# A feed-forward input product in seven block products instead of eight, for three double groups of hidden units

## The chip, the cores and the metric

The kernel runs on one NeuronCore of a Trainium2 chip. The time is the device time of one execution in microseconds, as the median of several runs. Five engines work from queues of their own, in order: TensorE (PE in the profile; its weight loads are PEld), VectorE (DVE), ScalarE (ACT), GpSimd (POOL) and SyncE (SP), which issues the loads.

## The reference

One layer of a decoder trunk on 256 tokens of width 1024, all in float32. After the mixing part and the cross attention over a memory comes the feed-forward part, which the change is about, and the final norm:

```python
def reference(...):
    ...
    h = h + memory_cross_attention(rmsnorm(h, norm_x_g[l]), rmsnorm(mem, norm_mem_g[l]),
                                   wq_x[l], wkv_x[l], wo_x[l])
    hn = rmsnorm(h, norm_ffn_g[l])
    gu = hn @ w_ffn_in[l]
    h = h + (jax.nn.silu(gu[..., :FFN_HIDDEN]) * gu[..., FFN_HIDDEN:]) @ w_ffn_out[l]
    return rmsnorm(h, final_norm_g)
```

`hn` is 256 x 1024, `w_ffn_in` 1024 x 5632, `w_ffn_out` 2816 x 1024.

## The kernel before, in words

All weights lie in one array of 1 MB units in the order in which they are used (`plan`, `ORDER`). A unit is 128 partitions by 2048 columns. For nearly full float32 accuracy every weight unit is split into two parts: `hi` is the value rounded by a copy on ScalarE, `lo = raw - hi` is a subtraction. `prep` does this for one unit: it issues the load on SP's queue (L188), the copy on ScalarE in two pieces of 1024 columns (L194), and the subtraction of each piece (L198), 576 columns of it on VectorE and 448 on GpSimd. Two raw buffers and three of each part are in rotation, and `nxt` prepares two units ahead. Activations are split in the same way (`split`, L285 and L286). A product then takes three matmuls for each 128 x 128 block of activations against 512 columns: hi by hi, hi by lo, lo by hi (`mm3t`, L238 to L240).

The feed-forward part works on 11 hidden groups of 256 units. Group `o` has two input units `("I", o, kh)`, one for each half of the 1024 features, with 256 columns of the gate and 256 of the value side by side, and one output unit `("O", o)`. `ffn_in` accumulates a bank of 128 tokens by 512 columns over both input units for each token half `t`: four block products of 12 matmuls for a group. `gate` takes Silu of the gate half (L1089, scaled by the token's reciprocal norm `r`) and multiplies (L1091, scaled by `r` again). `turn_hid` turns the result with four transposes into one bank (L1099) and splits it. `out_part` accumulates the output in four banks, 24 matmuls for an output unit. Output unit `o-1` runs behind the input of group `o`.

Ahead of that, the residual `H` gets the product with `wo` (`pso`, from four prepared units, the last two in buffers B10, B11, B12 and B6), `add_h` adds it and sums squares (L918, L922), and `turn_h2` turns a quarter of H (L1064), multiplies with the gain (L1066) and splits it, with the lo part on GpSimd (L1068). `rstd2` makes the reciprocal norms (L293, L295) and only the gates need them.

The order of TensorE's instructions is the program's. On ScalarE, VectorE, GpSimd and SP a planner orders the instructions by its own estimates; each engine's queue then runs strictly in that order, and an instruction at its head that waits holds back all behind it. Only the last part after the products has a written order.

Of the kernel before, what the change touches and what calls it, by code (L numbers as in the profile page):

```python
# [24 lines left out]
EPS = 1e-6  # L25
# [15 lines left out]
V_MIX, V_X, V_MEM, V_FFN, V_HG, V_L0, V_L1 = (8 * i for i in range(7))  # L41


def plan():
    order = []

    def tgroup(name, base):
        return [("T", name, base + c * 512, kh) for c in range(2) for kh in range(2)]

    order += [("T", "w_in", 4096 + c * 512, kh) for kh in range(2) for c in range(2)]  # L50
    order += [("F", "w_in", 3 * 1024 + c * 256) for c in range(4)]
    for base in (5, 2, 0, 1, 6):
        order += tgroup("w_in", base * 1024)
    order += tgroup("w_in", 8 * 1024) + tgroup("w_in", 7 * 1024)
    order += tgroup("w_br_hgrn", 0) + tgroup("w_br_attn", 0)
    order += tgroup("w_out", 0)
    order += [("F", "wkv_x", c * 256) for c in range(4)]
    order += tgroup("wkv_x", 1024)[:2]
    order += [("F", "wq_x", c * 256) for c in range(4)]
    order += tgroup("wkv_x", 1024)[2:]  # L60
    order += tgroup("wo_x", 0)
    for j in range(NF // 2):
        order += [("I", j, 0), ("I", j, 1)]
        if j:
            order.append(("O", j - 1))
    order.append(("O", NF // 2 - 1))
    return order


ORDER = plan()  # L70


def lay(ws):
# [39 lines left out]
def bc(ap, n, axis):  # L113
    shape = list(ap.shape)
    shape.insert(axis, n)
    return ap.unsqueeze(axis).to_broadcast(shape)


def build(tc, A, out):
    nc = tc.nc  # L120
    V, SC, G, PE, SY = nc.vector, nc.scalar, nc.gpsimd, nc.tensor, nc.sync
    with ExitStack() as ctx:
# [3 lines left out]
        cp = pool("cp", 1)  # L126
        wr, wh, wl = pool("wr", 2), pool("wh", 3), pool("wl", 3)
# [114 lines left out]
        def by_k(w, k):  # L242
            return tuple(t.rearrange("p (k c) -> p k c", k=k) for t in w)
# [671 lines left out]
        def add_h(t, c, ps, scale, ssq):  # L915
            d = H[:, t, c * 512:(c + 1) * 512]
            if scale is None:
                V.tensor_tensor(d, ps, d, op=ALU.add)  # L918
# [3 lines left out]
            SC.activation(j, d, AF.Square, accum_out=ssq[:, t, c:c + 1])  # L922
# [129 lines left out]
        gfin = big("B4", "gfin", (128, 1024))  # L1052
        SY.dma_start(gfin, A["gfin"].to_broadcast([128, 1024]))
        H2 = big("P2", "H2", (128, 2, 8, 256), F32R)
        h2h, h2l = H2[:, 0], H2[:, 1]
        def wo_part(ps, t, c, kh):
            t_part(ps, wo[2 * c + kh], (oxh, oxl), t, kh)

        def turn_h2(t, c):
            ks, ts = slice(4 * c, 4 * c + 4), slice(t * 128, (t + 1) * 128)  # L1060
            bk = bank("h2T", (128, 4, 128))
            for j in range(4):
                k = 4 * c + j
                PE.transpose(bk[:, j], H[:, t, k * 128:(k + 1) * 128], ident)  # L1064
            g = t2("h2g", (128, 4, 128))
            V.tensor_tensor(g, bk, bc(gv[:, V_FFN + 4 * c:V_FFN + 4 * c + 4], 128, 2), op=ALU.mult)  # L1066
            SC.activation(h2h[:, ks, ts], g, AF.Copy)
            G.tensor_tensor(h2l[:, ks, ts], g, h2h[:, ks, ts].bitcast(F32), op=ALU.subtract)  # L1068

        todo = None  # L1070
        for t in range(2):
            for c in range(2):
                ps = mm.tile([128, 512], F32, name="pso", tag="mm")
                wo_part(ps, t, c, 0)
                if todo:
                    turn_h2(*todo)
                wo_part(ps, t, c, 1)
                add_h(t, c, ps, None, ssq2)
                todo = (t, c)


        ring = ("B7", "B14", "B10", "B11", "B12", "B6")
        X2 = (h2h, h2l)
        hid, acc, two, psi, hm = {}, {}, {}, {}, {}

        def gate(o, t):
            r, ps = two["r"][:, t:t + 1], psi.pop((o, t))
            g = t2("fg", (128, 256))
            SC.activation(g, ps[:, 0:256], AF.Silu, scale=r)  # L1089
            u = t2b("fu", (128, 256))  # L1090
            V.scalar_tensor_tensor(u, ps[:, 256:512], r, g, op0=ALU.mult, op1=ALU.mult)  # L1091
            hm[o, t] = u

        def turn_hid(o):
            bk = mm.tile([128, 2, 256], F32, name="hidT", tag="mm")
            for t in range(2):
                u = hm.pop((o, t))
                for j in range(2):
                    PE.transpose(bk[:, j, t * 128:(t + 1) * 128], u[:, j * 128:(j + 1) * 128], ident)  # L1099
            hd = big(ring[o % 6], "hid", (128, 2, 2, 256), F32R)  # L1100
            split(bk, hd[:, 0], hd[:, 1])
            hid[o] = hd

        def ffn_in(o, kh, t, w):
            if kh == 0:
                psi[o, t] = mm.tile([128, 512], F32, name="psi", tag="mm")
            t_part(psi[o, t], w, X2, t, kh)
# [11 lines left out]
        def ffn_out(o):  # L1119
            w = by_k(nxt(), 2)  # L1120
            for t in range(2):
                for c in range(2):
                    out_part(o, w, t, c)

        for u in ORDER[at[0]:-2]:
            if u[0] == "O":
                ffn_out(u[1])
                continue
            _, o, kh = u
            w = by_k(nxt(), 4)  # L1130
            for t in range(2):
                ffn_in(o, kh, t, w)
                if (o, kh, t) == (0, 0, 0):
                    turn_h2(1, 1)
                    two["r"] = rstd2(ssq2, "h2")
                if kh == 1:
                    gate(o, t)
            if kh == 0 and o:
                turn_hid(o - 1)

        n = NF // 2 - 1
        wa = by_k(nxt(), 2)
        wb = by_k(nxt(), 2)
        out_part(n - 1, wa, 0, 0)
        turn_hid(n)
        out_part(n - 1, wa, 0, 1)
# [8 lines left out]


        ssq3 = cp.tile([128, 5], F32, name="ssq3")
        hg3 = {i: big(ring[j], "hg3", (128, 512)) for j, i in enumerate(((0, 0), (0, 1), (1, 0)))}  # L1160
# [95 lines left out]
```

## Time and profile before

| | |
|---|---|
| median of 3 runs | 624.86 us (624.67 to 625.35) |
| the profiled execution | 625.08 us, span 623.1 us, granted clock 0.998 |
| TensorE busy | 615.1 us, 99% |
| VectorE busy | 395.6 us, 63% |
| ScalarE busy | 334.1 us, 54% |
| GpSimd busy | 371.5 us, 60% |

A group's row gives the line, the engine, the operation, output and inputs, shapes, count, then the busy time in us and the mean duration in ns, and the idle time before it with what ended it. A row of the timeline gives start and duration in us. In the chain of waits each row is a start and the time that it adds to the chain. The feed-forward part begins at about 431 us of the span and its products end at 615.

### The profile page before, as it was taken

How to read it: one execution, taken by the hardware profiler on the slowest of the kernel's cores; microseconds unless marked ns; L12 is line 12 of the kernel's file. 1: busy time of each engine (PE TensorE's matmuls, PEld its weight loads, DVE VectorE, ACT ScalarE, POOL GpSimd, SP SyncE). 2: the span in 40 equal slices, each digit the busy share in tenths (PEclk: the TensorE clock that was granted, in tenths of full speed). 3: DMA queues.
4: the chain of work that ended last, by engine and by line, in shares of the span. 5: the costliest groups of instructions: out<-in, count | busy, mean ns of one | idle time of the engine just before them, and what ended most of it. 6: DMA issues, size and time to landing. Idle time of an engine off the chain costs nothing.

```text
span 623.1 us, 8546 instructions
## 1 busy us (share of the span) xinstructions
PE 615.1 (99%) x3153; PEld 513.7 (82%) x3153; DVE 395.6 (63%) x691; ACT 334.1 (54%) x550; POOL 371.5 (60%) x296
## 2 busy tenths in 40 slices
PE   8999999999999999999999999999999999999995
PEld 7888888888877877778888888888888888888884
DVE  7589888979776875748846456754444444444433
ACT  7785554234376866727547556644543344434432
POOL 3888744556544564356857876656655665566553
PEclk9999999999999999999999999999999999999999
DMA  8754553334433333545454544453354455455511
GB/s 346 288 197 149 203 202 136 136 135 147 191 137 135 136 136 136 203 174 191 145 213 189 187 176 178 143 196 135 136 180 175 187 202 184 177 184 198 204 68 68
DMA packets 16890, 107.53 MB, mean 173 GB/s; under 512 B 2000, under 2 KB 2640, under 8 KB 4560
## 3 DMA queue, kind: packets, MB, share of 16 engines
q1 hardware_dynamic: 16128, 106.14, 46.9%
q10 hardware_dynamic: 720, 0.84, 0.4%
q8 instruction: 25, 0.41, 0.3%
q14 instruction: 17, 0.14, 0.1%
HBM read 105.92 MB, written 1.05 MB: 172 GB/s over the span
## 4 chain that ended last, share of the span: by engine, by line
PE 98%; DVE 0%; POOL 0%; issue 0%; POOLq 0%; DVEq 0%
PE pst L238 13%; PE pst L240 13%; PE pst L239 13%; PE psf L259 7%; PE psi L238 6%; PE psi L240 6%; PE psi L239 6%; PE psf L260 4%; PE acc L240 3%; PE acc L238 3%; PE acc L239 3%; PE lp L613 2%; PE psg L514 1%; PE pso L238 1%; PE pso L240 1%; PE pso L239 1%
## 5 line engine op out<-in xcount | busy, mean ns | idle before, releaser
L198 POOL TENSOR_TENSOR lo<-raw,hi 128x448 fp32r<-128x448 f32 x172 | 272.0, 1597 | 181.4 <-ACT hi L194 178.4
L194 ACT ACTIVATE hi<-raw 128x1024 fp32r<-128x1024 f32 (+1 forms) x194 | 196.2, 1037 | 161.1 <-PE pst L240 58.2
L198 DVE TENSOR_TENSOR lo<-raw,hi 128x576 fp32r<-128x576 f32 (+2 forms) x194 | 197.8, 1024 | 127.9 <-ACT hi L194 126.1
L238 PE MATMUL pst<-hi,XX 128*128 128x512 f32 x224 | 90.4, 404 | 0.0
L240 PE MATMUL pst<-hi,XX 128*128 128x512 f32 x224 | 87.4, 390 | 0.0
L239 PE MATMUL pst<-lo,XX 128*128 128x512 f32 x224 | 87.3, 390 | 0.0
L238 PE MATMUL psi<-hi,H 128*128 128x512 f32 x176 | 69.6, 395 | 0.0
L240 PE MATMUL psi<-hi,H 128*128 128x512 f32 x176 | 68.7, 390 | 0.0
L239 PE MATMUL psi<-lo,H 128*128 128x512 f32 x176 | 68.5, 389 | 0.0
L240 PEld LDWEIGHTS pst<-hi,XX 128*128 128x128 f32 x224 | 42.0, 188 | 9.0
L238 PEld LDWEIGHTS pst<-hi,XX 128*128 128x128 f32 x224 | 42.1, 188 | 8.8 <-issue 0.7
L239 PEld LDWEIGHTS pst<-lo,XX 128*128 128x128 f32 x224 | 42.1, 188 | 7.9
L240 PEld LDWEIGHTS psi<-hi,H 128*128 128x128 f32 x176 | 33.0, 188 | 7.1
L239 PEld LDWEIGHTS psi<-lo,H 128*128 128x128 f32 x176 | 33.1, 188 | 6.6
L238 PEld LDWEIGHTS psi<-hi,H 128*128 128x128 f32 x176 | 33.1, 188 | 6.5
L238 PE MATMUL acc<-hi,hid 128*128 128x512 f32 x86 | 33.6, 390 | 0.0
L240 PE MATMUL acc<-hi,hid 128*128 128x512 f32 x86 | 33.5, 389 | 0.0
L239 PE MATMUL acc<-lo,hid 128*128 128x512 f32 x86 | 33.5, 389 | 0.0
L1091 DVE SCALAR_TENSOR_TENSOR fu<-psi,r_h,fg 128x256 f32<-128x256 f32 x22 | 10.6, 483 | 25.1 <-ACT fg L1089 25.1
L1089 ACT ACTIVATE fg<-psi,r_h 128x256 f32<-128x256 f32 x22 | 10.4, 475 | 29.1 <-PE psi L240 29.1
L259 PE MATMUL psf<-H,hi 128*128 128x512 f32 x64 | 22.8, 400 | 0.0
L259 PE MATMUL psf<-XX,hi 128*128 128x512 f32 x64 | 22.6, 396 | 0.0
(336 smaller groups left out, 1199.4 us busy)
## 6 DMA issues: line engine op xcount, KB each, us to landing
raw<-w SPq DMA_DIRECT2D x94, 1024.0 KB, 4.8
raw<-w SPq DMA_DIRECT2D x4, 512.0 KB, 6.5
raw<-w SPq DMA_DIRECT2D x4, 256.0 KB, 4.0
H<-xtok SPq DMA_DIRECT2D x1, 1024.0 KB, 9.6
mraw<-mT SPq DMA_DIRECT2D x1, 1024.0 KB, 4.9
xraw<-xT SPq DMA_DIRECT2D x1, 512.0 KB, 6.5
gfin<-gfin SPq DMA_DIRECT2D x1, 512.0 KB, 3.7
out<-H SPq DMA_DIRECT2D x2, 256.0 KB, 2.0
```

The source lines that it names most:

```text
L194: SC.activation(hi[:, a], raw[:, a], AF.Copy)
L198: eng.tensor_tensor(lo[:, b], raw[:, b], hi[:, b].bitcast(F32), op=ALU.subtract)
L238: PE.matmul(ps, xh, h, start=first, stop=False)
L239: PE.matmul(ps, xh, l, start=False, stop=False)
L240: PE.matmul(ps, xl, h, start=False, stop=last)
L259: PE.matmul(ps, w[0][:, k, a], X2[:, :, k], start=k == 0, stop=False)
L260: PE.matmul(ps[:, 0], w[1][:, k, a], X2[:, 0, k], start=False, stop=k == 7)
L514: PE.matmul(pss[c][t], z[:, k, t * 128:(t + 1) * 128], ws[c][0][:, k], start=z is Xh and k == 0, stop=False)
L613: PE.matmul(ps[:, j], KS[:, a0 + j], QQ[:, a0 + j], start=True, stop=True)
L1089: SC.activation(g, ps[:, 0:256], AF.Silu, scale=r)
L1091: V.scalar_tensor_tensor(u, ps[:, 256:512], r, g, op0=ALU.mult, op1=ALU.mult)
```

## The change

Two neighbouring hidden groups `q` and `q+1` form a double group; there are three (2 and 3, 5 and 6, 8 and 9). For such a pair the input product is two token halves by two feature halves by two groups, eight block products. The new code computes it with Winograd's form of Strassen's scheme: seven block products of sums of blocks. `SEVEN` gives their order, P1, P2, P6, P7, P5, P3, P4. Products with plain operands are P1 (block 11 by token half 0, feature half 0), P2 (block 21, feature half 1); the others use sums. The groups 0, 1, 4, 7 and 10 keep the old form.

- `load_blocks` loads the four blocks of a double group into the fixed buffers B12, B6, B10 and B11 and forms the combination of 22 and 12 at once; `block` forms three more combinations in place (for P6, P5, P4). Each combination is two VectorE operations of 1024 columns (`both`). `BY_DMA` is false, so `less` isn't used.
- `halve` splits a unit or a block in one piece of 2048 columns (two pieces for the first two units): copy on ScalarE, subtraction on VectorE alone. Every fourth goes to a fixed pair of buffers in P1's place (`px`). GpSimd splits no weights from here on. `prep_u` prepares three units ahead.
- `token_sums` forms four sums of token blocks and splits them, on VectorE with copies on ScalarE.
- `ffn_product` runs one product into one of three banks (A, B, F), and copies partial sums of bank A away on ScalarE (`keep`) where a later step needs them; `whole` adds a kept sum to a bank on VectorE.
- The reciprocal norm is applied ahead of the transposes (`rstd_h2`, `add_h2`), and not in `gate`; the lo part of the turned tokens moves to VectorE. The units 0 to 3 run first for token half 0, then for half 1, with the transposes of half 1 before unit 3.
- The output units are spread among the products by `ffn_plan`, the turns by `TURNS`.

```diff
+SEVEN = ("P1", "P2", "P6", "P7", "P5", "P3", "P4")
+def ffn_plan():
...
+    out = two(0) + two(1)
+    out += seven(2, P2=[0], P5=[1]) + two(4)
+    out += seven(5, P2=[2], P7=[3], P5=[4]) + two(7)
+    out += seven(8, P2=[5], P7=[6], P5=[7])
+    out += two(10) + [("O", 8)]
+    return out + [("O", 9), ("O", 10)]
...
+LOADS = {0: (2,), 10: (5,), 22: (8,)}
+TURNS = {4: (0,), 8: (1,), 15: (2,), 18: (3,), 20: (4,), 27: (5,), 30: (6,), 32: (7,), 38: (8, 9)}
...
+        def halve(raw, n):
+            if n % 4 == 3:
+                hi, lo = px[:, 0:2048], px[:, 2048:4096]
...
+                SC.activation(hi[:, a], raw[:, a], AF.Copy)
+                V.tensor_tensor(lo[:, a], raw[:, a], hi[:, a].bitcast(F32), op=ALU.subtract)
...
+        def block(q, name):
...
+            if name == "P6":
+                both(blk["11"], blk["12"], blk["11"], ALU.add)
+            elif name == "P5":
+                both(blk["12"], blk["22"], blk["11"], ALU.subtract)
+            elif name == "P4" and not BY_DMA:
+                both(blk["21"], blk["21"], blk["11"], ALU.subtract)
...
-            G.tensor_tensor(h2l[:, ks, ts], g, h2h[:, ks, ts].bitcast(F32), op=ALU.subtract)
+                V.tensor_tensor(h2l[:, ks, ts], g, h2h[:, ks, ts].bitcast(F32), op=ALU.subtract)
...
+        def token_sums():
+            a11, a12, a21, a22 = (h2g[t, c] for t in range(2) for c in range(2))
...
+            V.tensor_tensor(a22, a21, a22, op=ALU.add)
+            V.tensor_tensor(s2, a22, a11, op=ALU.subtract)
+            V.tensor_tensor(a21, a11, a21, op=ALU.subtract)
+            V.tensor_tensor(a12, a12, s2, op=ALU.subtract)
...
+            if name == "P1":
+                keep("1", ps, t2("f1"))
+            elif name == "P2":
+                whole(q, 0, ps, "1")
+            elif name == "P6":
+                keep("2", ps, gf[:, 1024:1536])
+            elif name == "P5":
+                keep("4", ps, gf[:, 1536:2048])
+                whole(q + 1, 1, bank_of["F"], "4")
+            elif name == "P3":
+                psi[q + 1, 0] = ps
+                gate(q + 1, 0)
+            elif name == "P4":
+                whole(q, 1, ps, "2")
...
+        prep_u(3)
+        for n in range(4):
+            if n == 3:
+                turn_h2(1, hn1)
+            ffn_in(n, 0)
+        for n in range(4):
+            for q in LOADS.get(n, ()):
+                load_blocks(q)
+            ffn_in(n, 1)
+            if n == 0:
+                token_sums()
+            prep_u(n + 4)
+        for n in range(4, len(units) - 2):
+            for q in LOADS.get(n, ()):
+                load_blocks(q)
+            prep_u(n + 3)
+            for o in TURNS.get(n, ()):
+                turn_hid(o)
...
```

More of the change, by code (lines that the diff above doesn't have):

```diff
@@ L70, with seven, two @@
 ORDER = plan()
+SEVEN = ("P1", "P2", "P6", "P7", "P5", "P3", "P4")
+def ffn_plan():
+    def seven(q, **after):
+        out = []
+        for p in SEVEN:
+            out.append(("P", q, p))
+            out += [("O", o) for o in after.get(p, ())]
+        return out
+    def two(j):
+        return [("I", j, 0), ("I", j, 1)]
+    out = two(0) + two(1)
[4 more added lines that the diff above has]
+    return out + [("O", 9), ("O", 10)]
+FFN_PLAN = ffn_plan()
+BY_DMA = False
+LOADS = {0: (2,), 10: (5,), 22: (8,)}
+TURNS = {4: (0,), 8: (1,), 15: (2,), 18: (3,), 20: (4,), 27: (5,), 30: (6,), 32: (7,), 38: (8, 9)}
 def lay(ws):
@@ new lines, in both, with load_blocks @@
+        def both(out, x, y, op):
+            for i in range(2):
+                a = slice(1024 * i, 1024 * i + 1024)
+                V.tensor_tensor(out[:, a], x[:, a], y[:, a], op=op)
+        def load_blocks(q):
+            blk.clear()
+            for key, tag, c in (("22", "B12", (q + 1, 1)), ("12", "B6", (q + 1, 0)),
+                                ("11", "B10", (q, 0)), ("21", "B11", (q, 1))):
+                blk[key] = big(tag, "b" + key, (128, 2048))
+                SY.dma_start(blk[key], A["w"][where[("I",) + c]])
+            if BY_DMA:
+                less(blk["12"], blk["12"], (q + 1, 1))
+            else:
+                both(blk["12"], blk["22"], blk["12"], ALU.subtract)
@@ new lines, in less @@
+        def less(out, x, c):
+            SC.activation(out, x, AF.Copy, scale=-1.0)
+            G.dma_start(out, A["w"][where[("I",) + c]], accum_op=ALU.add)
+        def block(q, name):
+            if name == "P7" and BY_DMA:
+                less(blk["21"], blk["11"], (q, 1))
+            if name == "P6":
[4 more added lines that the diff above has]
+                both(blk["21"], blk["21"], blk["11"], ALU.subtract)
+            return blk[{"P1": "11", "P2": "21", "P6": "11", "P7": "12", "P5": "12", "P3": "22", "P4": "21"}[name]]
@@ L1056, in wo_part, with prep_u @@
+        units = FFN_PLAN
+        def prep_u(upto):
+            while made_u[0] <= min(upto, len(units) - 1):
+                n = made_u[0]
+                made_u[0] += 1
+                u = units[n]
+                if u[0] == "P":
+                    raw = block(u[1], u[2])
+                else:
+                    raw = wr.tile([128, 2048], F32, name="raw", tag="raw")
+                    SY.dma_start(raw, A["w"][where[u]])
+                pair[n] = halve(raw, n)
         def wo_part(ps, t, c, kh):
@@ L1070, in build, with add_h2, rstd_h2 @@
-        todo = None
+        ssq2 = cp.tile([128, 4], F32, name="ssq2")
+        v2 = cp.tile([128, 2], F32, name="v2")
+        r2 = cp.tile([128, 2], F32, name="r2")
+        h2g = {}
+        def add_h2(t, c, ps):
+            d = H[:, t, c * 512:(c + 1) * 512]
+            V.tensor_tensor(d, ps, d, op=ALU.add)
+            SC.activation(t2b("hjunk"), d, AF.Square, scale=1.0 / 32.0, accum_out=ssq2[:, 2 * t + c:2 * t + c + 1])
+        def rstd_h2(t):
+            V.tensor_scalar(v2[:, t:t + 1], ssq2[:, 2 * t:2 * t + 1], ssq2[:, 2 * t + 1:2 * t + 2], EPS,
+                            op0=ALU.add, op1=ALU.add)
+            G.tensor_tensor(r2[:, t:t + 1], v2[:, t:t + 1], nhalf[:, :1], op=ALU.pow)
+            hn = []
+            for c in range(2):
+                n = t2("hn")
+                SC.activation(n, H[:, t, c * 512:(c + 1) * 512], AF.Copy, scale=r2[:, t:t + 1])
+                hn.append(n)
+            return hn
@@ L1071, in build @@
+        hn0 = None
         for t in range(2):
@@ L1117, in out_part, with ffn_in @@
                      (o == 0 or home is not None) and k == 0, k == 1 and o >= NF // 2 - (2 if t and c else 1))
-        def ffn_out(o):
-            w = by_k(nxt(), 2)
+        def ffn_in(n, t):
+            _, o, kh = units[n]
+            if kh == 0:
+                psi[o, t] = mm.tile([128, 512], F32, name="psi", tag="mm")
+            t_part(psi[o, t], by_k(pair[n], 4), X2, t, kh)
+            if kh == 1:
+                gate(o, t)
+        SS = big("P0", "SS", (128, 2, 4, 4, 128), F32R)
@@ new lines, in tokens, with product @@
+        def tokens(name):
+            if name in ("P1", "P2", "P4"):
+                t, kh = {"P1": (0, 0), "P2": (0, 1), "P4": (1, 1)}[name]
+                return [[z[:, 4 * kh + k, t * 128:(t + 1) * 128] for k in range(4)] for z in X2]
+            i = {"P5": 0, "P6": 1, "P7": 2, "P3": 3}[name]
+            return [[SS[:, z, i, k] for k in range(4)] for z in range(2)]
+        def product(ps, name, w, first):
+            xh, xl = tokens(name)
+            for k in range(4):
+                for i, (x, z) in enumerate(((xh, w[0]), (xh, w[1]), (xl, w[0]))):
+                    PE.matmul(ps, x[k], z[:, k], start=first and k == 0 and i == 0, stop=k == 3 and i == 2,
+                              skip_group_check=not first)
@@ new lines, in build, with keep, whole, ffn_product @@
+        bank_of, kept = {}, {}
+        def keep(key, ps, home):
+            SC.activation(home, ps, AF.Copy)
+            kept[key] = home
+        def whole(q, t, ps, key):
+            c = t2("fc")
+            V.tensor_tensor(c, ps, kept.pop(key), op=ALU.add)
+            psi[q, t] = c
+            gate(q, t)
+        def ffn_product(n):
+            _, q, name = units[n]
+            w = by_k(pair[n], 4)
+            key = {"P1": "A", "P6": "A", "P5": "A", "P3": "A", "P2": "B", "P7": "F", "P4": "F"}[name]
+            first = name in ("P1", "P2", "P7")
+            if first:
+                bank_of[key] = mm.tile([128, 512], F32, name="pq" + key, tag="mm")
+            ps = bank_of[key]
+            product(ps, name, w, first)
+            if name == "P1":
[12 more added lines that the diff above has]
+                whole(q, 1, ps, "2")
@@ L1121, in ffn_out @@
+        def ffn_out(n):
+            w = by_k(pair[n], 2)
             for t in range(2):
                 for c in range(2):
[L1123 to L1139, printed above, removed]
+                    out_part(units[n][1], w, t, c)
@@ new lines, in build @@
+        prep_u(3)
[16 more added lines that the diff above has]
+                turn_hid(o)
+            u = units[n]
+            if u[0] == "I":
+                for t in range(2):
+                    ffn_in(n, t)
+            elif u[0] == "P":
+                ffn_product(n)
+            else:
+                ffn_out(n)
@@ L1143, in build @@
         n = NF // 2 - 1
-        wa = by_k(nxt(), 2)
-        wb = by_k(nxt(), 2)
+        wa, wb = (by_k(pair[len(units) - 2 + i], 2) for i in range(2))
         out_part(n - 1, wa, 0, 0)
@@ L1159, in build @@
         ssq3 = cp.tile([128, 5], F32, name="ssq3")
-        hg3 = {i: big(ring[j], "hg3", (128, 512)) for j, i in enumerate(((0, 0), (0, 1), (1, 0)))}
+        hg3 = {i: big(tag, "hg3", (128, 512)) for tag, i in zip(("B10", "B11", "B12"), ((0, 0), (0, 1), (1, 0)))}
         v3 = cp.tile([128, 3], F32, name="v3")
```

81 lines of the change are left out of this document (50 added, 31 removed).

## The prediction

> **What bounds the kernel now.** I read the head of the page first, then the chain of waits, then single matmuls in the timeline.
>
> ```profile
> span 623.1 us, 8546 instructions
> PE 615.1 (99%) x3153; PEld 513.7 (82%) x3153; DVE 395.6 (63%) x691; ACT 334.1 (54%) x550; POOL 371.5 (60%) x296
> PE 98%; DVE 0%; POOL 0%; issue 0%; POOLq 0%; DVEq 0%
> ```
>
> TensorE carries 98% of the chain: a matmul less is time less, as long as its operands are there in time. How much is one matmul?
>
> ```profile
> L239 PE MATMUL psi<-lo,H 128*128 128x512 f32 x176 | 68.5, 389 | 0.0
> 598.21 0.39 PE L240 MATMUL psi<-hi,H 128*128 128x512 f32 x1
> 598.89 0.39 PE L240 MATMUL psi<-hi,H 128*128 128x512 f32 x1
> 448.10 0.44 PE hidT L1099 x4
> 464.89 0.44 PE hidT L1099 x4
> 448.10:464.90 16.80, 16.80 (x78) 13.92 (x77) 7.68 (x9) 7.35 (x9) 10.03 (x6) 1.00 0.53 188
> ```
>
> The group row says 389 ns, but matmuls overlap: three starts lie between 598.21 and 598.89, so one costs 0.227 us. One hidden group of the feed-forward lasts 448.10 to 464.89, 16.79 us, which is 72 matmuls and four transposes (0.44): again 0.227. In that window (columns: length, then PE, PEld, DVE, ACT, POOL busy) VectorE works 7.68 of 16.80 us and the granted clock is 1.00. So before the change VectorE has more than half of its time free there. That is the reserve that the change spends.
>
> **The saving.** A double group takes eight block products of 12 matmuls now and seven after: 3 x 12 = 36 matmuls fewer (the build of both kernels has 2226 and 2190 matmuls 512 wide). 36 x 0.227 = 8.2 us off the chain. By the durations it would be 36 x 0.389 = 14.0, which the pitch refutes. Transposes stay at 44 and 16.
>
> **What VectorE gets.** Durations and the pitch between them:
>
> ```profile
> L198 DVE TENSOR_TENSOR lo<-raw,hi 128x1024 fp32r<-128x1024 f32 x2 | 2.4, 1216 | 0.0
> L286 DVE TENSOR_TENSOR hid<-hidT,hid 128x512 fp32r<-128x512 f32 x11 | 7.5, 685 | 1.4 <-ACT hid L285 1.4
> L286 DVE TENSOR_TENSOR oal<-ao,oah 128x256 fp32r<-128x256 f32 x8 | 3.3, 417 | 0.0
> 449.28 0.76 DVE L198 TENSOR_TENSOR lo<-raw,hi 128x576 fp32r<-128x576 f32 x1 [2.75 <-ACT hi L194]
> 449.95 0.68 DVE L286 TENSOR_TENSOR hid<-hidT,hid 128x512 fp32r<-128x512 f32 x1
> L198 DVE TENSOR_TENSOR lo<-raw,hi 128x576 fp32r<-128x576 f32 x172 | 174.3, 1016 | 123.4 <-ACT hi L194 121.7
> ```
>
> From 512 to 1024 columns 685 grows to 1216 ns, 1.04 ns a column; 2048 columns, which no run shows, come to 1216 + 1024 x 1.04 = 2.28 us. The 576-wide split takes 0.76 us alone at 449.28 but 1016 ns in the mean, where GpSimd splits beside it; after the change GpSimd splits nothing there, so I take the undisturbed values. Queued instructions overlap: 449.95 starts 0.67 us after a start of 0.76 us, so 0.08 to 0.09 less. Pitches: 2048 wide 2.20, 1024 wide 1.14, 512 wide 0.605, 256 wide 0.34.
>
> I then counted VectorE's queue in the build's order. In a double group it splits 7 products, 2 or 3 output units and 2 ordinary input units, and forms four block combinations (eight halves of 1024). From the first product of groups 5-6 to that of 8-9: 12 x 2.20 + 8 x 1.14 + 6 x 0.605 (three hidden splits, three sums with a kept bank) + 6 x 0.34 (gates) = 41.2 us, against 204 matmuls and 12 transposes on TensorE, 46.3 + 1.3 = 47.6. Between the first products of 2-3 and 5-6 it is 38 against 41.7. VectorE is the second engine everywhere, with 86 to 92% of TensorE's work, and in order.
>
> **Where it becomes the first: the opening.** The stretch begins when TensorE has turned the second token half (before unit 3), and ends with the lo part of the second hidden group, which the third matmul of output unit 1 reads. VectorE's queue there holds, without a gap in which it could wait for less: 8 splits of 2048 (17.6), 8 half combinations (9.1), 15 of 512 (two gains, two token splits, four token sums and their four splits, two hidden splits, one kept sum: 9.1) and 4 gates (1.4): 37.2 us, and about 0.5 where an instruction waits for the result of the one ahead. TensorE's work in it is 146 matmuls and 8 transposes: 33.1 + 0.9 = 34.0. The difference, 3.7 us, must appear as TensorE idling, most of it at P5 and at output unit 1, because the build puts hidden split 1 behind three block splits. After each stall the first matmul starts cold:
>
> ```profile
> 599.48 0.48 PE L238 MATMUL psi<-hi,H 128*128 128x512 f32 x1
> 599.79 0.40 PE L239 MATMUL psi<-lo,H 128*128 128x512 f32 x1
> ```
>
> Behind the transposes the first start takes 0.31 instead of 0.23, so three stalls add some 0.3. Term: +4.0. Bounds: 0, if TensorE's operands in fact never depend on the last of this queue; 6.8, if queued instructions did not overlap (35 x 0.08 = 2.8 more). I stay at the queue sum, since the overlap stands in the rows.
>
> The Trainium skill, in VectorE: DVE Perf Modes, section The DRAIN you can't avoid, says that the next operation does not start before the pipe of the last is empty. The trace disagrees by the 0.08 us shown.
>
> **What is hidden.** The rstd now stands ahead of the transposes instead of in the gate:
>
> ```profile
> 431.32 0.69 DVE L918 TENSOR_TENSOR H<-pso,H 128x512 f32<-128x512 f32 x1 [1.62 <-PE pso L240]
> 432.11 0.63 ACT L922 ACTIVATE hjunk<-H 128x512 f32<-128x512 f32 x1 [1.74 <-DVE H L918]
> 433.31 0.70 POOL L295 TENSOR_TENSOR r_h<-v__4128,nhalf 128x2 f32<-128x2 f32 x1 [0.83 <-DVE v__4128 L293]
> 443.07 1.05 ACT L194 ACTIVATE hi<-raw 128x1024 fp32r<-128x1024 f32 x1
> ```
>
> For the second token half: add 0.69, square with its readout 0.8, sum 0.17, power 0.70, two scalings 1.3, handovers: 4.1 us; unit 3's split stands ahead of it on ScalarE (2048 wide, 1.9 from 1.05 for 1024) and on VectorE (2.2), so up to 6.5. Cover: three half units of 12 matmuls, 8.2 us. Nothing, and 1 to 2 us if unit 3's load comes late. The first half has 5.4 us of matmuls over 4.1. ScalarE: 42 splits x 1.8 and some 30 copies and gates more, about 105 us of the stage's 176: not the bound. GpSimd loses 66 splits, off the chain: 0. Keeping P1, P6, P5 takes three copies a double group on ScalarE, each behind one product or output unit (2.7 us and more): 0.
>
> **Loads.** Same bytes, but a double group's four blocks go to fixed buffers, freed late and in a burst.
>
> ```profile
> q1 hardware_dynamic: 16128, 106.14, 46.9%
> raw<-w SPq DMA_DIRECT2D x94, 1024.0 KB, 4.8
> SPq L188 <- DVE lo L198: 461.4, 90, 12.7
> ```
>
> 106.14 MB took 46.9% of 623.1 us, 292 us: 2.9 us per 1 MB load at full rate, and 4.8 with the 1.9 of a lone load's latency. At the opening blocks 22 and 12 follow the last matmul of wo: 12 lands 7.7 us after it, its combination is due 10.1 us after it (three half units, transposes, two gains). In the later groups the fifth load of the burst is wanted after some 16 to 18 us and lands after 5 x 2.9 + 1.9 = 16.4. Term 0, by 2 us or less of margin. What waits behind: VectorE's combination holds back everything after it in the queue, and SP's queue, which already waits for VectorE's splits (461.4 us in 90 waits), holds the next units' loads.
>
> **Sum.** The profiled execution took 625.08 us (span 623.1): 625.08 - 8.2 + 4.0 = 620.9. It lay 0.22 above the median of 624.86, so 620.7. The tail is the old one.
>
> **Rivals.**
> A, the forecast: 620.7, own range 618.5 to 623.3.
> B, the queue is longer than summed: no overlap (2.8 more) or waits for the wrong thing in later groups too: 623.5 to 625.5. For it: one in-order queue holds TensorE-dependent gates ahead of splits. Against it: the 5 us and more of room per later group. By the skill's DRAIN sentence above, 35 starts lose 0.08 each and the time is 623.5; the rows give that little weight.
> C, slower: the blocks come late. If the loads of a burst land 4.8 us apart instead of 2.9, the fifth lands at 25.9, 8 to 10 us late in each of the two later groups, of which VectorE's and the unit lead's room takes about half, and the opening's combination 1.6 late: 620.7 + 1.6 + 2 x 4.5 = 631. It decides from about 3.7 us a load, where the lateness eats the 4.2 us net. For it: fixed buffers, and a combination that needs two loads at once. Against it: the 2.9 of the queue's row.
> D, the stall is hidden: 616.7, the saving alone. For it: a unit's first matmul needs no lo part, and the stretch could start with work done ahead. Against it: nothing in the queue before the stretch's end can be left for later.
> E, not seven products: excluded by the count of matmuls.
>
> **Chances.** A 0.55, B 0.17, C 0.18, D 0.10. A measurement of this kernel tells about 0.2%, 1.25 us, from no change: 623.6 to 626.1. Faster: A, D and a fifth of B, 0.68; same: most of B and a little of C, 0.13; slower: the rest, 0.19. The range reaches from near D into C, 617 to 628.
>
> **What to look at afterwards.** 2190 matmuls 512 wide at a pitch of 0.227. VectorE's 2048-wide split at 2.28 us, its share near nine tenths in the feed-forward's first 45 us. TensorE idle in two or three places before output unit 1, about 4 us together, ended by VectorE's hidden split or ScalarE's copy of P5's block, and next to none in groups 5-6 and 8-9. If the blocks' DMA ends waits of VectorE, C is right; if a 2048-wide split lies well over 2.3 us, a contention that the rows of before don't show makes the prediction wrong.

## The result

The changed kernel takes 620.15 us (median, 619.96 to 620.55); the kernel before, on the same chip, takes 625.11 us (624.67 to 625.41). The ratio is 0.9922, 95% interval 0.9905 to 0.9939: 5.0 us or 0.8% faster. The forecast was 620.7. The profiled execution took 619.96 us.

The head of the page after, its engine row, and the first row of the chain of waits:

```profile
span 618.2 us, 8376 instructions
PE 607.5 (98%) x3117; PEld 506.7 (82%) x3117; DVE 460.0 (74%) x714; ACT 355.2 (57%) x545; POOL 256.5 (41%) x227
PE 89%; DVE 7%; issue 1%; ACT 1%; DMA 1%; POOL 0%; POOLq 0%; DVEq 0%; ACTq 0%
```

There are 36 matmuls fewer (3153 to 3117 records). VectorE goes from 395.6 to 460.0 us of work and from 0% to 7% of the chain, GpSimd from 371.5 to 256.5. Nearly 6% of the 7% is one stretch, 439 to 477 us, shown below; the other 1% lies just ahead of and in the `wo` product. First VectorE's two most frequent new forms in the groups of the feed-forward part, and the loads of the blocks (median us from issue to landing):

```profile
L1099 DVE TENSOR_TENSOR lo<-raw,hi 128x2048 fp32r<-128x2048 f32 x17 | 38.9, 2290 | 8.0 <-ACT hi L1098 7.9
L1106 DVE TENSOR_TENSOR b<-b,b 128x1024 f32<-128x1024 f32 x24 | 28.5, 1219 | 0.0
```
```profile
b<-w SPq DMA_DIRECT2D x12, 1024.0 KB, 5.9
```

The 2048-wide split takes 2.29 us (forecast 2.28). The idle time of `b<-b` is 0.0: no combination of blocks waited for a load. Now the windows of the opening and of two stretches behind it, with the columns of the prediction's window row:

```profile
435.00:477.00 42.00, 39.62 (x180) 31.99 (x179) 38.13 (x38) 27.87 (x29) 0.56 (x1) 1.00 0.45 179
477.00:524.60 47.60, 47.60 (x217) 39.37 (x217) 42.20 (x33) 26.89 (x24) 0.00 (x0) 1.00 0.59 230
524.60:571.00 46.40, 46.40 (x212) 38.42 (x211) 40.86 (x32) 27.33 (x24) 0.00 (x0) 1.00 0.40 148
```

VectorE fills nine tenths of each, but TensorE is short of work in the opening alone. Where it stops there is seen best in the timeline of its weight loads, which carry the waits of the matmuls behind them. These are all the waits over 0.15 us from the `wo` product to the last product:

```profile
410.45 0.19 PEld L265 LDWEIGHTS pso<-hi,ox 128*128 128x128 f32 x1 [0.25 <-DVE ox L311]
412.18 0.19 PEld L265 LDWEIGHTS pso<-hi,ox 128*128 128x128 f32 x1 [0.51 <-DVE ox L311]
459.68 0.19 PEld L265 LDWEIGHTS acc<-hi,hids 128*128 128x128 f32 x1 [0.44 <-DVE hids L311]
471.60 0.19 PEld L1269 LDWEIGHTS pqA<-hi,SS 128*128 128x128 f32 x1 [1.11 <-ACT gf L1275]
476.76 0.19 PEld L265 LDWEIGHTS acc<-hi,hids 128*128 128x128 f32 x1 [2.09 <-DVE hids L311]
```

A weight load runs ahead of its matmul, so TensorE itself loses less than the brackets say. By the starts of the matmuls, less the pitch of 0.227, and with what the first matmul behind each stop takes longer until the next can start (0.10 to 0.12), the three waits of the opening cost 0.28, 0.96 and 1.93 us, together 3.17. The two in the `wo` product cost 0.46. Groups 5-6 and 8-9 have none.

**A measure for the stage.** The instructions ahead of the `wo` product are the same in both kernels, but the product does not start at the same time. The timeline of TensorE, before and then after, at a first product of the mixing part (`psf`) and at the `wo` product (`pso`):

```profile
28.66 0.48 PE L259 MATMUL psf<-XX,hi 128*128 128x512 f32 x1
...
407.89 0.40 PE L238 MATMUL pso<-hi,ox 128*128 128x512 f32 x1
```
```profile
28.21 0.47 PE L284 MATMUL psf<-XX,hi 128*128 128x512 f32 x1
...
407.26 0.40 PE L263 MATMUL pso<-hi,ox 128*128 128x512 f32 x1
```

I therefore compare profiled executions by span less the start of that product, and call this the stage. Before it is 623.1 - 407.89 = 215.2 us, after 618.2 - 407.26 = 210.9: 4.3 us less, where the medians differ by 5.0. The terms: 36 matmuls at 0.227 take off 8.2; the opening gives back 3.2 and the `wo` product 0.5. That is -4.5, 0.2 more than measured. Between the `wo` product and the end no other two starts of matmuls lie further apart than in the kernel before; small differences of first matmuls, transposes and the tail, 0.1 to 0.3 each and of both signs, are not read finer than that.

### The profile page after: what moved, and what is told of

Its sections match the earlier page's. It is cut to its first block, busy times and chain, and to the rows that moved or that the text cites. A ratio compares the mean times of both kernels' runs of the same rounds, so it can differ in the third digit from the quotient of the medians.

```text
span 618.2 us, 8376 instructions
## 1 busy us (share of the span) xinstructions
PE 607.5 (98%) x3117; PEld 506.7 (82%) x3117; DVE 460.0 (74%) x714; ACT 355.2 (57%) x545; POOL 256.5 (41%) x227
## 4 chain that ended last, share of the span: by engine, by line
PE 89%; DVE 7%; issue 1%; ACT 1%; DMA 1%; POOL 0%; POOLq 0%; DVEq 0%; ACTq 0%
PE pst L263 13%; PE pst L265 13%; PE pst L264 13%; PE psf L284 7%; PE pqA L1269 4%; PE psf L285 4%; PE acc L265 3%; PE acc L263 3%; PE acc L264 3%; DVE lo L1099 2%; PE psi L263 2%; PE psi L265 2%; PE pqF L1269 2%; PE psi L264 2%; PE lp L638 2%; DVE b L1106 1%
## 5 line engine op out<-in xcount | busy, mean ns | idle before, releaser
L223 POOL TENSOR_TENSOR lo<-raw,hi 128x448 fp32r<-128x448 f32 x106 | 161.7, 1540 | 110.6 <-ACT hi L219 107.8
L219 ACT ACTIVATE hi<-raw 128x1024 fp32r<-128x1024 f32 (+1 forms) x128 | 128.7, 1028 | 93.7 <-PE pst L265 58.1
L223 DVE TENSOR_TENSOR lo<-raw,hi 128x576 fp32r<-128x576 f32 (+2 forms) x128 | 131.1, 1031 | 57.2 <-ACT hi L219 54.2
L1099 DVE TENSOR_TENSOR lo<-raw,hi 128x2048 fp32r<-128x2048 f32 (+1 forms) x21 | 43.7, 2086 | 12.2 <-ACT hi L1098 12.1
L1098 ACT ACTIVATE hi<-raw 128x2048 fp32r<-128x2048 f32 (+1 forms) x21 | 36.6, 1750 | 16.4 <-issue 5.6
L1099 DVE TENSOR_TENSOR lo<-b,hi 128x2048 fp32r<-128x2048 f32 x13 | 29.8, 2289 | 8.0 <-ACT hi L1098 8.0
L265 PE MATMUL acc<-hi,hids 128*128 128x512 f32 x78 | 30.7, 393 | 1.7 <-DVE hids L311 1.7
L263 PE MATMUL acc<-hi,hids 128*128 128x512 f32 x78 | 30.7, 393 | 0.0
L264 PE MATMUL acc<-lo,hids 128*128 128x512 f32 x78 | 30.4, 390 | 0.0
L263 PE MATMUL psi<-hi,H 128*128 128x512 f32 x72 | 28.1, 391 | 0.0
L265 PE MATMUL psi<-hi,H 128*128 128x512 f32 x72 | 28.1, 390 | 0.0
L264 PE MATMUL psi<-lo,H 128*128 128x512 f32 x72 | 28.0, 389 | 0.0
```

What stands on the lines that cost most here:

```text
L219: SC.activation(hi[:, a], raw[:, a], AF.Copy)
L223: eng.tensor_tensor(lo[:, b], raw[:, b], hi[:, b].bitcast(F32), op=ALU.subtract)
L263: PE.matmul(ps, xh, h, start=first, stop=False)
L264: PE.matmul(ps, xh, l, start=False, stop=False)
L265: PE.matmul(ps, xl, h, start=False, stop=last)
L1098: SC.activation(hi[:, a], raw[:, a], AF.Copy)
```

## The experiments

In each diff a minus is the changed kernel, which the text also calls "after". "Stage" is as above.

**Is VectorE the bound in the opening, and nowhere else?** Two kernels subtract one lo part twice, 2.2 us more of VectorE's work: once in the first double group, once in the third. The result of the subtraction is the same.

```diff
-                V.tensor_tensor(lo[:, a], raw[:, a], hi[:, a].bitcast(F32), op=ALU.subtract)
+                for _ in range(2 if n == 4 else 1):
+                    V.tensor_tensor(lo[:, a], raw[:, a], hi[:, a].bitcast(F32), op=ALU.subtract)
```

> The lo part of P1's block in the first double group is subtracted twice, one more VectorE instruction of 2048 columns in the opening (2.2 us). Theory (the opening is bound by VectorE's queue, one for one): the time rises by 2.2 us over the changed kernel, to about 622.4, and the idle time of TensorE before output unit 1 grows by as much. Rival (the idle time comes from which instruction stands where, with room elsewhere in the queue): a rise of less than 1 us.

With `n == 27` for the third group:

> The same second subtraction, for P1's block of the third double group. Theory (VectorE has some 5 us of room per later group): no rise, 620.2 within 0.4. Rival (VectorE's queue is the bound in every double group): a rise of about 2.2 us, to 622.4.

The first took 623.02 us (ratio to before 0.9963, 0.995 to 0.9975), stage 212.8, 1.9 more than after; the medians differ by 2.9, of which the later start of its `wo` product (408.37) accounts for 1.1. The other took 620.56 (0.993, 0.9917 to 0.9942), stage 210.9, no change. The weight loads' waits in the opening, with the split doubled there:

```profile
455.22 0.20 PEld L1216 LDWEIGHTS hidT<-cst,fu 128*128 128x128 f32 x2 [1.00 <-DVE fu L1209]
462.82 0.19 PEld L265 LDWEIGHTS acc<-hi,hids 128*128 128x128 f32 x1 [1.66 <-DVE hids L311]
474.74 0.19 PEld L1270 LDWEIGHTS pqA<-hi,SS 128*128 128x128 f32 x1 [1.12 <-ACT gf L1276]
479.91 0.19 PEld L265 LDWEIGHTS acc<-hi,hids 128*128 128x128 f32 x1 [2.12 <-DVE hids L311]
```

What is added ahead of output unit 0 is waited for there; the last two waits stay as they were. In the opening VectorE's work added at this place costs nearly one for one, in a later double group 2.2 us are free.

**What does the first double group earn?** Groups 2 and 3 go back to the plain form; the other two double groups stay.

```diff
-    out = two(0) + two(1)
-    out += seven(2, P2=[0], P5=[1]) + two(4)
-    out += seven(5, P2=[2], P7=[3], P5=[4]) + two(7)
+    out = two(0) + two(1) + two(2) + [("O", 0)] + two(3) + [("O", 1)] + two(4) + [("O", 2)]
+    out += seven(5, P2=[3], P5=[4]) + two(7)
-LOADS = {0: (2,), 10: (5,), 22: (8,)}
-TURNS = {4: (0,), 8: (1,), 15: (2,), 18: (3,), 20: (4,), 27: (5,), 30: (6,), 32: (7,), 38: (8, 9)}
+LOADS = {8: (5,), 19: (8,)}
+TURNS = {4: (0,), 7: (1,), 10: (2,), 13: (3,), 16: (4,), 24: (5,), 27: (6,), 29: (7,), 35: (8, 9)}
```

> The groups 2 and 3 keep the old form; seven products for 5-6 and 8-9 only. 24 matmuls are saved instead of 36, 5.4 us instead of 8.2. Theory (all the loss lies in the first double group): the opening's 3.2 us of idle time go with it, and the time is 625.1 - 5.4 + 0.4 (the wo stage's two stalls) = 620.1, no slower than with three. Rival (each double group loses a third of it): 625.1 - 2/3 x 5.0 = 621.8.

620.08 us (0.9916, 0.9902 to 0.9929), as forecast; stage 210.3, 4.9 under before. 24 matmuls are 5.4, less the 0.5 of the `wo` product's stops: 5.0. So the pitch prices a removed matmul; and the first double group, whose 12 matmuls are worth 2.7, pays 3.2 in stops and is worth less than nothing (its stage is 0.6 longer).

**All three pairs later.** The double groups become 3-4, 6-7 and 9-10, so that three plain groups and an output unit stand ahead.

```diff
-    out = two(0) + two(1)
-    out += seven(2, P2=[0], P5=[1]) + two(4)
-    out += seven(5, P2=[2], P7=[3], P5=[4]) + two(7)
-    out += seven(8, P2=[5], P7=[6], P5=[7])
-    out += two(10) + [("O", 8)]
-    return out + [("O", 9), ("O", 10)]
+    out = two(0) + two(1) + two(2) + [("O", 0)]
+    out += seven(3, P2=[1], P5=[2]) + two(5)
+    out += seven(6, P2=[3], P7=[4], P5=[5]) + two(8)
+    out += seven(9, P2=[6], P5=[7])
+    return out + [("O", 8), ("O", 9), ("O", 10)]
-LOADS = {0: (2,), 10: (5,), 22: (8,)}
-TURNS = {4: (0,), 8: (1,), 15: (2,), 18: (3,), 20: (4,), 27: (5,), 30: (6,), 32: (7,), 38: (8, 9)}
+LOADS = {3: (3,), 13: (6,), 25: (9,)}
+TURNS = {4: (0,), 7: (1,), 9: (2,), 17: (3,), 18: (4,), 20: (5,), 29: (6,), 30: (7,), 32: (8,)}
...
+                if t == 0 and units[n][1] == 8:
+                    turn_hid(9)
```

> Three double groups still, but 3-4, 6-7 and 9-10: two input units and output unit 0 run between the opening and the first product, and the blocks are loaded three units later. Theory (the opening asks 37.4 us of VectorE for 34.0 us of TensorE; with 16 us of ordinary units in it, it asks for less than TensorE's time): nearly the whole saving appears, 625.1 - 8.2 + 0.5 = 617.4. Rival (the first double group loses its 3 us wherever it stands): 620.

619.23 us (0.9903, 0.9888 to 0.9918), 1.8 over what I expected. The stops of the opening are gone, but these are left, beside 0.24 and 0.50 in the `wo` product:

```profile
507.77 0.20 PEld L1214 LDWEIGHTS hidT<-cst,fu 128*128 128x128 f32 x2 [0.18 <-DVE fu L1207]
595.76 0.20 PEld L1214 LDWEIGHTS hidT<-cst,fu 128*128 128x128 f32 x2 [0.79 <-DVE fu L1207]
```

The transposes of two hidden groups wait for a gate, the longer time those of group 9. By the starts TensorE loses 0.8 us at these two places; the stops of the `wo` product were in the expectation. Another 0.5 lies behind the products: the output's transfer on ScalarE's queue lands 3.0 us after its issue instead of 2.2 in the changed kernel, in this kernel and nearly so (2.9) in the next; why is not known. That is 1.3 of the 1.8. The next kernel keeps this plan, moves that turn behind three quarters of output unit 8, and gives GpSimd its old share of the first two units' splits.

```diff
-                V.tensor_tensor(lo[:, a], raw[:, a], hi[:, a].bitcast(F32), op=ALU.subtract)
+                cut = (c + 1) * w - (POOL_COLS // 2 if n < 2 else 0)
+                for eng, b in ((V, slice(c * w, cut)), (G, slice(cut, (c + 1) * w))):
+                    if b.start < b.stop:
+                        eng.tensor_tensor(lo[:, b], raw[:, b], hi[:, b].bitcast(F32), op=ALU.subtract)
...
+                    if units[n][1] == 8 and (t, c) == (1, 0):
+                        turn_hid(9)
```

> As the kernel with the late double groups (3-4, 6-7, 9-10), with two stalls of its trace taken away: the turn of hidden group 9 stands after three quarters of output unit 8 instead of two (TensorE waited 0.79 us for its gate), and the splits of the units 0 and 1 give GpSimd its old share, so that VectorE reaches the last two attention splits earlier (0.5 and 0.24 us in front of the wo product). Theory: 1.2 us less than the late kernel's 619.2, so 618.0. Rival (what is saved there is lost at the next wait): 619.2.

617.69 us (0.9881, 0.9868 to 0.9895), stage 208.0: as forecast, and faster than both kernels. Of all waits of weight loads over 0.15 us from the `wo` product on, one is left:

```profile
507.42 0.20 PEld L1217 LDWEIGHTS hidT<-cst,fu 128*128 128x128 f32 x2 [0.50 <-DVE fu L1210]
```

This also shows what the stops in the `wo` product were: without GpSimd's share, VectorE splits 1024 columns of unit 0 (1.23 us, against 0.76 here and before) ahead of the attention output `ox`, which TensorE needs next.

**Can GpSimd take work back?** It stands nearly idle in the opening (0.56 us). First the lo parts of the four token sums:

```diff
-                V.tensor_tensor(SS[:, 1, i], g, SS[:, 0, i].bitcast(F32), op=ALU.subtract)
+                G.tensor_tensor(SS[:, 1, i], g, SS[:, 0, i].bitcast(F32), op=ALU.subtract)
```

> The changed kernel, but the lo parts of the four token sums are made on GpSimd: four instructions of 512 columns (2.4 us) leave VectorE's queue in the opening. Theory (the opening is VectorE's queue, one for one, and GpSimd's work does not disturb it): 2.4 us less idle time of TensorE there, 617.8. Rival (GpSimd and VectorE slow each other, as the 576-wide split that took 0.76 us alone and 1.44 beside GpSimd suggests): VectorE's other instructions lengthen by about 2 us while GpSimd works, and the time stays at 620 to 620.5.

623.69 us (0.9975, 0.9966 to 0.9985): 3.5 more than after, against every expectation; the stage, 213.4, is 2.5 longer. Its timeline, VectorE's rows and then GpSimd's:

```profile
446.46 1.79 DVE L1255 TENSOR_TENSOR h2g<-h2g,s 128x512 f32<-128x512 f32 x1
448.18 2.28 DVE L1099 TENSOR_TENSOR lo<-b,hi 128x2048 fp32r<-128x2048 f32 x1
...
450.71 1.99 DVE L1106 TENSOR_TENSOR b<-b,b 128x1024 f32<-128x1024 f32 x1
452.63 3.37 DVE L1099 TENSOR_TENSOR lo<-b,hi 128x2048 fp32r<-128x2048 f32 x1
455.92 3.38 DVE L1099 TENSOR_TENSOR lo<-raw,hi 128x2048 fp32r<-128x2048 f32 x1
...
472.17 2.29 DVE L1099 TENSOR_TENSOR lo<-b,hi 128x2048 fp32r<-128x2048 f32 x1 [0.93 <-ACT hi L1098]
```
```profile
445.96 1.74 POOL L1246 TENSOR_TENSOR SS<-h2g,SS 128x512 fp32r<-128x512 f32 x1 [9.99 <-ACT SS L1245]
448.29 3.33 POOL L1246 TENSOR_TENSOR SS<-s,SS 128x512 fp32r<-128x512 f32 x1 [0.58 <-ACT SS L1245]
451.58 5.56 POOL L1246 TENSOR_TENSOR SS<-h2g,SS 128x512 fp32r<-128x512 f32 x2
```

Four GpSimd instructions, four slowed VectorE instructions. Of 512, 1024 and twice 2048 columns, they take 1.10, 0.77, 1.08 and 1.09 us longer than in the changed kernel (0.69, 1.22, 2.29): an amount for each meeting, not a share of the length. The last one fits a turn-taking: it needs 2.29 us and ends at 459.30, so it got going at 457.01, and GpSimd's pair ends at 457.14. It works the other way too: the VectorE split at 448.18 is undisturbed, and GpSimd's at 448.29 takes 3.33 us and ends at 451.62, about 1.2 after VectorE's end. VectorE saves 4 x 0.605 = 2.4 us and loses 4.0, and at P5's block it now waits 0.93 us for ScalarE: together the stage's 2.5. The other 1.0 of the medians lies outside the stage. The Trainium skill, SBUF — State Buffer, section SBUF: two separate sides, has this rule: VectorE instructions with two inputs in SBUF and GpSimd instructions that read SBUF hold a pair of ports in turn, whole instructions at a time. The four rows agree with it, and a slowdown in proportion would not give the same 1.1 us for 512 and 2048 columns.

Then GpSimd's old share (896 of 2048 columns) of every split:

```diff
-                V.tensor_tensor(lo[:, a], raw[:, a], hi[:, a].bitcast(F32), op=ALU.subtract)
+                cut = (c + 1) * w - POOL_COLS // pieces
+                for eng, b in ((V, slice(c * w, cut)), (G, slice(cut, (c + 1) * w))):
+                    eng.tensor_tensor(lo[:, b], raw[:, b], hi[:, b].bitcast(F32), op=ALU.subtract)
```

> The changed kernel, but every split of a weight unit or block gives GpSimd 896 of the 2048 columns, the share it had before. By the rows of before (576 columns of VectorE in 1016 ns beside GpSimd's 448 in 1597) a split takes VectorE 2.0 us instead of 2.2 and GpSimd 3.2. Theory (side by side the two gain little): the eight splits of the opening take 1.4 us less of VectorE, but each lo part comes about 1 us later; 618.5 to 621.5. Rival (VectorE's part halves): the opening's idle time goes, 617.

645.28 us (1.0326, 1.0312 to 1.0341), an expectation missed by 24 us. From the groups of the same part of the span, and one window:

```profile
L1108 DVE TENSOR_TENSOR b<-b,b 128x1024 f32<-128x1024 f32 x24 | 39.8, 1682 | 2.5 <-DMA b<-w 2.5
L1101 DVE TENSOR_TENSOR lo<-raw,hi 128x1152 fp32r<-128x1152 f32 x16 | 34.0, 2133 | 5.8 <-ACT hi L1098 5.8
L1101 POOL TENSOR_TENSOR lo<-raw,hi 128x896 fp32r<-128x896 f32 x16 | 44.7, 2796 | 23.2 <-ACT hi L1098 23.2
```
```profile
477.00:524.60 47.60, 36.42 (x146) 28.91 (x147) 45.24 (x28) 26.24 (x23) 31.19 (x11) 0.93 0.50 177
```

A VectorE split of 1152 columns takes 2.13 us in this group, hardly less than one of 2048 alone (2.29). The combinations, which nobody shares, go from 1.22 to 1.68. So handing over 44% of such a split saves 0.16 us of it and lengthens the combinations. TensorE works 36.4 of 47.6 us in the second window, and the stops reach the later groups: the waits of weight loads over 0.15 us add up to 22.5 us, the longest 5.44 for a gate in the second double group. The mended kernel shares the splits of the first two units alone, and no stop shows there.

**Is the opening a pure queue?** My forecast took the sum of VectorE's instructions. A kernel with `BY_DMA` set forms two of the four combinations of a double group by a negating copy on ScalarE and an adding load, and so takes 4 x 1.14 = 4.6 us of that sum away.

```diff
-BY_DMA = False
+BY_DMA = True
```

> The changed kernel with its other branch: two of the four block combinations of each double group are formed by a negating copy on ScalarE and a load that adds the other block on arrival. VectorE's queue in the opening loses four instructions of 1024 columns (4.6 us): 32.8 us against TensorE's 34.0. Theory (VectorE's queue alone is what is short): the opening's idle time goes, 617. Rival (the negating copy of 1.9 us waits for its block, the adding load takes a lone load's 4.8 us after it, and the combination is wanted about 2.4 us after its blocks have landed): the combined block comes 4 us or more late, the instructions behind it wait too, and the time is 621 or more.

619.95 us (0.9919, 0.9905 to 0.9932), between the two expectations; stage 210.1, 0.8 less than after, where the medians differ by 0.2. The wait of 0.44 is gone, the other two stay (0.85 and 1.97 on the weight loads). VectorE's timeline there:

```profile
465.52 1.22 DVE L1106 TENSOR_TENSOR b<-b,b 128x1024 f32<-128x1024 f32 x1
468.79 2.29 DVE L1099 TENSOR_TENSOR lo<-b,hi 128x2048 fp32r<-128x2048 f32 x1 [2.05 <-ACT hi L1098]
```

The same place in the changed kernel, VectorE and then ScalarE:

```profile
439.27 1.29 DVE L1179 TENSOR_TENSOR h2g<-h2T,gv 128x512 f32<-128x512 f32 x2
...
466.00 3.50 DVE L1106 TENSOR_TENSOR b<-b,b 128x1024 f32<-128x1024 f32 x3
469.41 2.29 DVE L1099 TENSOR_TENSOR lo<-b,hi 128x2048 fp32r<-128x2048 f32 x1
471.61 2.29 DVE L1099 TENSOR_TENSOR lo<-raw,hi 128x2048 fp32r<-128x2048 f32 x1
473.81 2.29 DVE L1099 TENSOR_TENSOR px<-b,px 128x2048 fp32r<-128x2048 f32 x1
476.02 0.69 DVE L311 TENSOR_TENSOR hids<-hidT,hids 128x512 fp32r<-128x512 f32 x1
```
```profile
467.34 1.92 ACT L1098 ACTIVATE hi<-b 128x2048 fp32r<-128x2048 f32 x1 [2.21 <-DVE b L1106]
469.17 1.90 ACT L1098 ACTIVATE hi<-raw 128x2048 fp32r<-128x2048 f32 x1
470.97 0.57 ACT L1275 ACTIVATE gf<-pqA 128x512 f32<-128x512 f32 x1
```

Of the three `b<-b` at 466.00, the first completes P5's block. ScalarE needs 1.9 us for its hi part, and VectorE fills just that time with P4's combination (the other two). Taken away, they leave VectorE waiting 2.05 us; with three shorter waits for ScalarE (0.87, 0.20 and 0.34) 3.5 of the 4.6 us come back as waiting. The adding loads land 10.9 us (median) after their issue, but nothing in the opening waits for them. The rows show both late waits. P5's bank A is free only when ScalarE has copied P6's sum to `gf`, and that copy stands behind two splits of 1.9. The hidden split `hids` at 476.02 stands behind three splits of 2.2.

So the same work in another order: hidden group 1 is turned one unit earlier.

```diff
-TURNS = {4: (0,), 8: (1,), 15: (2,), 18: (3,), 20: (4,), 27: (5,), 30: (6,), 32: (7,), 38: (8, 9)}
+TURNS = {4: (0,), 7: (1,), 15: (2,), 18: (3,), 20: (4,), 27: (5,), 30: (6,), 32: (7,), 38: (8, 9)}
```

> Hidden group 1 is turned one unit earlier, so that its split stands ahead of the three block splits on VectorE; VectorE's work in the opening stays the same to the instruction. Theory 1 (the opening is a pure queue: its length decides): the sum of the queue is unchanged, the stall of 2.1 us at output unit 1 only moves to the next block product, and the time stays at 620.1 (619.7 to 620.6). Theory 2 (the stall at output unit 1 is one of order: the hidden split is ready late only because three splits of 2.2 us stand ahead of it, and the blocks behind have room): the stall of 2.1 us goes, P5's of 1.1 stays or grows by up to 0.6 since ScalarE copies the hidden split ahead of P5's block, and the time is 618.2 to 618.9.

618.99 us (0.99, 0.9887 to 0.9914), stage 209.4, 1.5 less than after: the second theory, 0.1 above its range. The waits of weight loads in the opening:

```profile
460.28 0.19 PEld L265 LDWEIGHTS acc<-hi,hids 128*128 128x128 f32 x1 [0.44 <-DVE hids L311]
472.18 0.19 PEld L1269 LDWEIGHTS pqA<-hi,SS 128*128 128x128 f32 x1 [1.09 <-ACT gf L1275]
472.96 0.19 PEld L1269 LDWEIGHTS pqA<-lo,SS 128*128 128x128 f32 x1 [0.60 <-DVE lo L1099]
```

The wait of 2.09 is gone, and 0.60 of a new one has come at P5's lo part, one hidden split later than before. With VectorE's work the same, half of the opening's cost was order.

**Does the early difference belong to the kernel?** The changed kernel once more:

> The changed kernel once more, with nothing edited. It tells whether the start of the wo product, which lay between 407.3 and 408.5 us in kernels with the same instructions up to there, belongs to the kernel as built or to the single execution. If it belongs to the build, this run shows 407.3 again, as the changed kernel did; if to the execution, it lies anywhere between 407.2 and 408.5. The time is expected at 620.1 (619.6 to 620.7), the stretch from the wo product to the end at 210.9.

620.37 us (0.9923, 0.991 to 0.9937). Its profiled execution was its longest, 622.19 us: the span is 620.4, and TensorE's timeline has

```profile
30.55 0.47 PE L284 MATMUL psf<-XX,hi 128*128 128x512 f32 x1
...
409.58 0.40 PE L263 MATMUL pso<-hi,ox 128*128 128x512 f32 x1
```

The `wo` product starts 2.3 us later than in the first profile of the same program, outside both expected ranges, and the stage is 210.8 against 210.9. So the difference belongs to the execution, and it is there at 30 us already: 30.55 against 28.21.

## Why the prediction was right, and where it was not

- **The saving, -8.2: right.** The two-double-group kernel prices 24 removed matmuls as the pitch does.
- **The durations: right.** 2.28 was 2.29. Queued instructions overlap as taken: the split at 473.81 follows the one at 471.61 by 2.20, at a duration of 2.29. The sentence that would have made it 623.5 (the Trainium skill, VectorE: DVE Perf Modes, section The DRAIN you can't avoid) does not fit these rows when it is taken alone. The same section goes on that a next operation that is not held starts earlier, so the rows do not contradict the section, contrary to what the prediction says. One reading was loose: the 0.76 us at 449.28 were not "alone", since a GpSimd split started at 449.38. It was VectorE's turn there; where GpSimd's split started first, at 444.25, VectorE's at 445.10 took 1.44. So the trace of before already held the turns that the GpSimd experiments met.
- **The opening, +4.0: right in size, 3.2 measured; its reason only in part.** The step "the difference, 3.7 us, must appear as TensorE idling" took the queue's length for the cause. VectorE does run from 439.27, the first gain after the transposes, to 476.71, the end of `hids`: 37.4 us for a forecast 37.7. And work added ahead of output unit 0 costs nearly one for one. But 4.6 us taken away gave 0.8, and a new order with the same work 1.5, measured in the stage. The sum was the right size because the last instruction that TensorE needed stood at the end of the queue, and that was a choice of order. The sentence against rival D, "nothing in the queue before the stretch's end can be left for later", is the one that failed: two of the three block splits could be at no cost, and the first, P5's, at 0.6 us.
- **"Keeping P1, P6, P5 ... 0": wrong by up to 1.0.** The keep of P6 does come behind a product of 2.7 us, but on ScalarE two splits (3.7 us) stand ahead of it, and P5 waits for its bank. How much of the 0.96 would go if the keep stood first was not tried; P5's lo part, which its second matmul needs, is ready at 471.70, 0.2 us after the bank, so I'd expect little.
- **The `wo` product, not in the sum: +0.46.** I counted GpSimd's loss of 66 splits as off the chain. For the first two units it put 448 columns a piece onto VectorE ahead of `ox`. The mended kernel, which gives that share back, has no stop there.
- **No stop in the later groups, loads 0: right.** Windows 2 and 3 show TensorE full; 2.2 us more in the third group cost nothing; no combination waited for a block, although a block's median load took 5.9 us. Rival C's late blocks did not occur.
- **The hidden steps** (rstd ahead of the transposes, ScalarE's load) show no wait over 0.15 us.

The forecast sum of -4.2 stands against -4.3 in the stage. That it agrees so closely is in part luck: the opening was put 0.8 too high, and the 0.5 of the `wo` product was not in the sum. The median fell by 5.0 in one comparison and 4.8 in the other; the 0.4 to 0.7 between lie outside the stage. The start of the `wo` product differs by 2.3 us between two executions of one program, more than that, so I assign them to no part of the change.

Rival D's 616.7 was not excluded by the work but by its order: 617.7 was reached with the same seven products, started later and with GpSimd's old share of the first two units.

## What to carry to other kernels

Sum an in-order queue to find where an engine becomes the bound, but then ask which instruction of it the bound engine needs last, and whether that one could stand earlier: here one such move took 1.2 us off the time, and starting the products three groups in, with the first units' splits shared again, 2.5. A removed matmul is worth its start-to-start pitch and an instruction added in a stretch of slack nothing; both could be read from the profile of before. Before moving two-input work from VectorE to an idle GpSimd, look for VectorE instructions beside it: each meeting cost 0.8 to 1.1 us for a 512-wide GpSimd split.

## What the hardware showed that I had not expected

- GpSimd and VectorE take turns. A 512-wide GpSimd split delays a VectorE instruction by 0.8 to 1.1 us whatever its width; sharing every split of a weight unit or block made the kernel 3.3% slower than before.
- The same program started its `wo` product at 407.3 us in one execution and at 409.6 in another, and the difference is there at 30 us. Its cause stays open. A gain of less than 1 us is better read from a stage than from two spans.
- In the kernel with shared splits the granted clock of a window fell to 0.93, with TensorE working 36 of 47.6 us; in the changed kernel it was 1.00 in all three windows. Whether the pauses cause it was not tried.
- The first matmul behind a stop takes 0.10 to 0.12 us more until the next can start, as after transposes (0.08 to 0.09).
